# The input halves of the projections in one tile, two of eight pieces on the weights' place modulo 256 bytes

## The chip, the cores and the metric

The kernel runs on one core of a Trainium2 chip. The metric is the device time of one execution in microseconds; a measurement gives the median of several executions of the kernel before and of the kernel after on the same chip.

## The reference

Two transformer blocks are chained on a sequence of 256 tokens with 1024 features. The first has one layer: a mixer (gated delta rule and an S5 state-space model), cross-attention to a memory of 256 tokens, a SwiGLU feed-forward. The second has two layers: a self-attention (stick-breaking and MoBA heads in the first, forgetting attention in the second), a cross-attention to a second memory, a feed-forward with a short convolution. Cut to what the change touches:

```python
def memory_cross_attention(h, mem_h, w_q, w_kv, w_out):
    q = (h @ w_q).reshape(B, S, XA_HEADS, XA_HEAD_DIM)
    kv = (mem_h @ w_kv).reshape(B, M, 2, XA_HEADS, XA_HEAD_DIM)
    k, v = kv[:, :, 0], kv[:, :, 1]
    s = jnp.einsum('bshd,bmhd->bhsm', q, k).astype(jnp.float32) * (XA_HEAD_DIM ** -0.5)
    p = jax.nn.softmax(s, axis=-1).astype(h.dtype)
    o = jnp.einsum('bhsm,bmhd->bshd', p, v).reshape(B, S, XA_DIM)
    return o @ w_out

def conv_ffn(h, w_up, conv_w, conv_b, w_down):
    u = h @ w_up
    ...
    gate, val = c[..., :D_FF_2], c[..., D_FF_2:]
    return (jax.nn.silu(gate) * val) @ w_down
```

Everything is float32, and each block ends in a normalization.

## The kernel before

**Products in two halves.** A float32 product is made of three faster ones: each operand is split into a high half, rounded to the matmul's own float32 format (F32R), and a low half, the rest. `mm3` issues high by high, high by low, low by high into one accumulator. The normalized input of a layer is held by feature: eight pieces of 128 features by 256 tokens, in the tiles xh and xl (`new_x`, L466; `split_x` fills them piece by piece). Weights come from memory as 512 KB pieces (raw), ScalarE writes their high half (whi), VectorE their low half (wlo); `Weights.pump` keeps four such pairs ahead in the pool "weights", and from the second block on three more in "weights2" (L1685).

**Projections.** `proj_f` runs over the eight pieces k, with the weights as the operand held in TensorE and the pieces of xh and xl streamed: 24 matmuls of 128x256. `proj_t`, for the values, turns it round: the weights are streamed, the halves of x held.

```python
for k in range(KD):
    mm3(p, wh[:, k], wl[:, k], N.xh[:, k], N.xl[:, k], k == 0, k == KD - 1)
```

`out_mm` (L576) is the same product for output projections: oh and ol (an attention's result), ahl (a feed-forward's) or xh and xl (the mixer's, kept in x tiles) are streamed. A feed-forward part runs 22 times over gate (24 matmuls), up (24) and down (24). In the trace a row names the streamed operand first: mm<-xh,whi streams xh against whi.

**Places.** Within the 256-byte rows of a partition, xh, xl, the memory's halves (memh, meml, mem2h, mem2l), ahl, oh and ol start 128 bytes past a multiple of 256; each piece is 1024 bytes, so all pieces do. whi and wlo start 192 past it. So in projections and output products the streamed operand lies 64 bytes before the weights, modulo 256; in `proj_t` it is 64 behind. On the same place (distance 0) lie three kinds of products: the S5 gate (s5ghl at 192, against whi; 48 matmuls), the cross-attention's result (PT with xvh and xvl, all at 128; 48) and its scores (Q, K, lb and V, all at 128; 48). The tiles v1 (192 bytes in the pool main), "beside" and "beside2" set the starts of what follows them in their pools.

**Softmax.** `softmax` works on one head's scores in PSUM: VectorE takes the negative maximum (nm, L1536), in the memory attention also multiplied by the rows' scale (nm<-nm,rs), ScalarE the exponential with its sum (sm), VectorE the reciprocal (rc, L1546) and the scaling of P (L1548). `softmax_pair` does two heads at once. nm, sm and rc have three buffers each. `memory_attention` issues its steps in the order of a list, MEMORY: s0 to s3 are the heads' scores with their softmax, t the transposes, v the values' products, p the products with the values, w one piece of weights ahead. The order on each engine comes out of a list scheduler, under the limits that the buffers set.

Of the kernel before, what the change touches and what calls it, by code (L numbers as in the profile page):

```python
# [10 lines left out]
F32 = mybir.dt.float32  # L11
F32R = mybir.dt.float32r
# [7 lines left out]
S = 256  # L20
KD = D // 128
# [11 lines left out]

MEMORY = "s0 w1 s1 w1 s2 w1 s3 w1 v0 t0 w1 v1 t1 w1 p0 t2 w1 p1 x0 t3 w1 p2 p3 x1".split()

XK_AT = [("v", 1), ("z", 0), ("z", 1), ("z", 1)]
EPS = 1e-6
PI = math.pi
# [149 lines left out]
def behind(tc, later, earlier):  # L188

    tc.add_manual_dep(later, earlier.name, mybir.DependencyInfo(  # L190
        mybir.DependencyClass.NoSync, mybir.DependencyReason.DATA), reason="order")
# [38 lines left out]
def body(ctx, tc, I, out):  # L230
# [5 lines left out]
    const = ctx.enter_context(tc.tile_pool(name="const", bufs=1))  # L236
    wpool = ctx.enter_context(tc.tile_pool(name="weights", bufs=1))
    main = ctx.enter_context(tc.tile_pool(name="main", bufs=1))
    small = ctx.enter_context(tc.tile_pool(name="small", bufs=2))
    W = Weights(nc, wpool, 4, 4, lambda a, b: behind(tc, a, b))  # L240

    v1 = main.tile([128, 48], F32, name="v1")


    def cols(w, c0, c1):
        return w.rearrange("(k p) n -> p k n", p=128)[:, :, c0:c1]
# [6 lines left out]
    for nm in "ukqvz":  # L253
        for c in range(2):
            W.add((nm, c), cols(w_in, OFFS[nm] + 256 * c, OFFS[nm] + 256 * c + 256), split=nm not in "uk")
            for x, at in enumerate(XK_AT):
                if at == (nm, c):
# [58 lines left out]
    def mm():  # L316
        return bank("mm", banks["mm"])
# [8 lines left out]
    def halves(p):  # L326
        return p.rearrange("p (a s) -> p a s", a=2)
# [133 lines left out]
    N = State()  # L461
    N.pending = []
    N.by_feature = True
    N.last = None

    def new_x():  # L466
        N.xh = main.tile([128, KD, S], F32R, name="xh", tag="xh", bufs=1)
        N.xl = main.tile([128, KD, S], F32R, name="xl", tag="xl", bufs=1)

    def split_x(n, src, gcol):  # L470
        a = A.activation(N.xh[:, n], src[:, n], AF.Copy, scale=gcol)
# [114 lines left out]
    def residual(accs, gcol, fold=None, by_feature=True):  # L586


        h = hn = N.h
        N.by_feature = by_feature  # L590
        new_x()
        if fold is not None:
            gg = small.tile([128, KD], F32, name="gg", tag="gg", bufs=1)
# [104 lines left out]
    def layer_cols():  # L698
        for nm in ("mix", "xa", "mem", "ffn"):
            for l in range(2):  # L700
                COL[nm, l] = COL[nm + "2"][:, KD * l:KD * l + KD]

    N.h = hT = main.tile([128, KD, S], F32, name="h", tag="h", bufs=1)
    new_x()
    def transpose_in(dst, src, evac, bank):
        for kp in range(4):
# [39 lines left out]
    def tt(o, a, b, op):  # L746
        N.v = V.tensor_tensor(o, a, b, op=op).ins  # L747
# [558 lines left out]
    def fill(n=1):  # L1306
        for _ in range(n):
            if fills:
                fills.pop(0)()
# [77 lines left out]
    for n in range(4):  # L1387
        p = mm()
# [5 lines left out]
        if n == 1:  # L1394
            split_x32()
        W.pump(1)
    fin_v(lambda i, n: v1[:, 0:n] if i else const.tile([128, n], F32, name="v0"))
    layer_cols()
    mixed = []

    def mix():
        if not mixed:
            new_x()
            mixed.extend([N.xh, N.xl])
        return mixed
# [40 lines left out]
    def dn_step(i):  # L1446
        if dn.left and i >= dn.least:
            with lane("dn"):
                dn.least = next(dn_gen, None)
            if dn.least is None:  # L1450
                dn.left = False
# [17 lines left out]
    for i in range(18):  # L1469
# [7 lines left out]
        if i < 16:  # L1477
            nm, n = todo[i]
            p = mm()
# [9 lines left out]
        if i % 2:  # L1489
            fill(2 * XK_AT.count((nm, n // 2)) if i < 16 else 0)  # L1490
        dn_step(i)
# [13 lines left out]
    for c in (2, 3, 0):  # L1505
        for kk in range(2):
            k = 2 * c + kk
# [11 lines left out]


    pm = ctx.enter_context(tc.tile_pool(name="second", bufs=1))
    pm.tile([128, 32], F32, name="beside")
    kvT = pm.tile([128, 2, S], F32, name="kvT")
    kvv = pm.tile([128, 2, S], F32, name="kvv")

# [4 lines left out]
    def softmax(p, parts, rs=None):  # L1530

        P = pm.tile([128, 512], F32, name="P", tag="P", bufs=2)
        nm = small.tile([128, 2], F32, name="nm", tag="nm", bufs=3)
        sm = small.tile([128, 2], F32, name="sm", tag="sm", bufs=3)
        if parts[0].stop - parts[0].start == parts[1].stop - parts[1].start:
            V.tensor_reduce(nm, halves(p), axis=AX.X, op=OP.max, negate=True)  # L1536
        else:
            for t, q in enumerate(parts):
                V.tensor_reduce(nm[:, t:t + 1], p[:, q], axis=AX.X, op=OP.max, negate=True)
        if rs is not None:  # L1540
            tt(nm, nm, rs, OP.mult)
        for t, q in enumerate(parts):
            A.activation(P[:, q], p[:, q], AF.Exp, bias=nm[:, t:t + 1], accum_out=sm[:, t:t + 1],
                         scale=1.0 if rs is None else rs[:, t:t + 1])
        rc = small.tile([128, 2], F32, name="rc", tag="rc", bufs=3)
        V.reciprocal(rc, sm)  # L1546
        for t, q in enumerate(parts):
            TS(P[:, q], P[:, q], rc[:, t:t + 1], None, op0=OP.mult)  # L1548
        return P

    def softmax_pair(p):

        P = pm.tile([128, 2, 384], F32, name="P", tag="P", bufs=2)
        nm = small.tile([128, 2, 2], F32, name="nm4", tag="nm4", bufs=3)
        sm = small.tile([128, 2, 2], F32, name="sm4", tag="sm4", bufs=3)
        for t in range(2):
            V.tensor_reduce(nm[:, t], p[t], axis=AX.X, op=OP.max, negate=True)
        for t, q in enumerate(CAUSAL):
            for i in range(2):
                A.activation(P[:, i, q], p[t][:, i], AF.Exp, bias=nm[:, t, i:i + 1], accum_out=sm[:, t, i:i + 1])  # L1560
        rc = small.tile([128, 2, 2], F32, name="rc4", tag="rc4", bufs=3)
        V.reciprocal(rc, sm)
        for t, q in enumerate(CAUSAL):
            for i in range(2):
                TS(P[:, i, q], P[:, i, q], rc[:, t, i:i + 1], None, op0=OP.mult)
        return P
# [81 lines left out]
    def x_scores(i):  # L1648
        p = full_scores([(qs[i][a][:, c], ks[i][b][c]) for c in range(2) for a, b in ((0, 0), (0, 1), (1, 0))])
        if i == 0:  # L1650
            flush()
            w_["rs"] = row_scale(1.0 / 16)
        Ps[i] = softmax(p, FULL, w_["rs"])
# [29 lines left out]
    residual(accs, COL["ffn"])  # L1683
    px_cm.__exit__(None, None, None)
    W.more = (ctx.enter_context(tc.tile_pool(name="weights2", bufs=1)), 3)  # L1685
    W.more[0].tile([128, 16], F32, name="beside2")
    padded = ctx.enter_context(tc.tile_pool(name="padded", bufs=1))
    W.nextra = 2
    W.extra = lambda: main.tile([128, 2048], F32, name="raw4", tag="m8", bufs=3)
# [192 lines left out]
    class Group:  # L1882


        def __init__(self, l, g, kind):
            self.l, self.g, self.kind = l, g, kind
            self.w = {}
            self.bank = acc if g < 3 else mm
# [130 lines left out]
    def memory_attention(l, gcol):  # L2019
# [17 lines left out]
        def score(h):  # L2037
            c, r = head(h)
            w["P", h] = softmax(full_scores([(w["q"][r, c], kvT[r, c])], acc), FULL, rs)
# [110 lines left out]
    v = small.tile([128, 2], F32, name="var", tag="var", bufs=2)  # L2150
    TS(v, ps[:, 0:2], 1.0 / D, EPS, op0=OP.mult, op1=OP.add)
    r = rsqrt_small(v, 2, A)
    for t in range(2):
        o = main.tile([128, D], F32, name="ofin", tag="m8", bufs=3)
# [31 lines left out]
```

## Time and profile before

| | |
|---|---|
| three executions | 1195.25, 1197.91, 1200.18 us (median 1197.91) |
| the profiled execution | 1196.38 us |
| its span, first to last instruction | 1194.6 us |
| TensorE (PE) busy | 97% of the span |
| VectorE, ScalarE, GpSimd busy | 75%, 56%, 6% |
| share of the chain that ended last on PE | 83% |

Matmuls are pipelined: a row's 0.28 us is the stay of one matmul in the engine, and the next one starts about 0.11 us after it. What a matmul costs in a stretch is therefore the distance of starts. The column PEclk is the clock that TensorE was granted, as a share of 2.4 GHz.

### The profile page before, as it was taken

To read this page: it belongs to the slowest core of one execution; us is meant where nothing else is said; L and a number is where in the kernel's file an instruction comes from. 1 tells how busy PE (TensorE), PEld (TensorE's weight loads), DVE (VectorE), ACT (ScalarE), POOL (GpSimd) and SP (SyncE) were. 2 spreads that over 40 slices of the span, in tenths; PEclk is the share of its full clock that TensorE was granted. 3 is DMA by queue.
4 is the path that set the end of the run, shared out by engine and by line. 5 is a ranking of instruction groups with operands and counts; after the bars stand their busy time and mean duration, and the time that the engine had idled before them with its cause. 6 is when DMAs were issued, how large, how long until landed. Compare 5 with 4: busy or idle time off the path is not lost.

```text
span 1194.6 us, 24101 instructions
## 1 busy us (share of the span) xinstructions
PE 1156.8 (97%) x9720; PEld 1102.7 (92%) x9720; DVE 891.8 (75%) x1682; ACT 667.1 (56%) x1155; POOL 77.1 (6%) x175
## 2 busy tenths in 40 slices
PE   8999998999999999999998999999999999999998
PEld 6798888999999999988797999999988888999998
DVE  8899747866875565877876899877765686978775
ACT  6553345655644444756665665655454666655653
POOL 1425300100000000200000000000100000000000
PEclk9999899999999999999999999999999999999998
DMA  8733352746665665653353576665543464666530
GB/s 207 198 83 109 98 159 63 220 150 188 194 198 169 195 198 163 185 169 118 105 168 113 162 208 194 195 212 158 145 140 116 143 172 137 179 190 195 176 90 36
DMA packets 262017, 188.01 MB, mean 157 GB/s; under 512 B 20143, under 2 KB 246852, under 8 KB 261906
## 3 DMA queue, kind: packets, MB, share of 16 engines
q1 hardware_dynamic: 258034, 185.23, 52.9%
q8 instruction: 76, 1.25, 0.4%
q10 hardware_dynamic: 3568, 0.86, 0.3%
q0 software_dynamic: 304, 0.39, 0.3%
q14 instruction: 35, 0.29, 0.1%
HBM read 183.70 MB, written 2.75 MB: 156 GB/s over the span
## 4 chain that ended last, share of the span: by engine, by line
PE 83%; DVE 7%; DMA 4%; ACT 2%; issue 1%; POOL 1%; SPq 0%; ACTq 0%; DVEq 0%; POOLq 0%
PE mm L536 16%; PE mm L537 16%; PE mm L538 16%; PE acc L582 7%; PE acc L584 7%; PE acc L583 7%; DVE wlo L157 1%; PE acc L1995 1%; DMA raw<-in_w_in_dram 1%; DVE s5a L747 1%; DVE ca L1110 1%; PE acc L1866 1%; DMA s5u<-uT 1%; DMA raws<-in_w_out_dram 1%; ACT whi L137 1%
## 5 line engine op out<-in xcount | busy, mean ns | idle before, releaser
L157 DVE TENSOR_TENSOR wlo<-raw,whi 128x1024 fp32r<-128x1024 f32 x322 | 392.0, 1226 | 149.6 <-ACT whi L137 147.3
L137 ACT ACTIVATE whi<-raw 128x1024 fp32r<-128x1024 f32 x322 | 337.0, 1057 | 285.6 <-PE mm L537 106.2
L536 PE MATMUL mm<-xh,whi 128*128 128x256 f32 x1504 | 421.3, 281 | 2.3 <-ACT V L218 1.4
L537 PE MATMUL mm<-xl,whi 128*128 128x256 f32 x1504 | 420.1, 280 | 0.0
L538 PE MATMUL mm<-xh,wlo 128*128 128x256 f32 x1504 | 419.7, 279 | 0.0
L536 PEld LDWEIGHTS mm<-xh,whi 128*128 128x128 f32 x1504 | 283.4, 189 | 4.3 <-ACT V L218 1.5
L537 PEld LDWEIGHTS mm<-xl,whi 128*128 128x128 f32 x1504 | 282.8, 188 | 1.5 <-issue 1.0
L538 PEld LDWEIGHTS mm<-xh,wlo 128*128 128x128 f32 x1504 | 283.6, 189 | 0.3
L584 PE MATMUL acc<-ahl,wlo 128*128 128x256 f32 x528 | 144.8, 279 | 0.4 <-DVE wlo L157 0.4
L583 PE MATMUL acc<-ahl,whi 128*128 128x256 f32 x528 | 144.9, 279 | 0.0
L582 PE MATMUL acc<-ahl,whi 128*128 128x256 f32 x528 | 141.7, 279 | 0.2 <-ACT ahl L218 0.2
L584 PEld LDWEIGHTS acc<-ahl,wlo 128*128 128x128 f32 x528 | 99.2, 189 | 0.8 <-DVE wlo L157 0.8
L583 PEld LDWEIGHTS acc<-ahl,whi 128*128 128x128 f32 x528 | 98.9, 188 | 0.0
L582 PEld LDWEIGHTS acc<-ahl,whi 128*128 128x128 f32 x528 | 97.2, 189 | 0.5 <-ACT ahl L218 0.5
L1740 DVE SCALAR_TENSOR_TENSOR gu<-pad,cwc,gu 128x256 f32<-128x256 f32 x176 | 75.1, 478 | 3.4 <-ACT gu L218 3.4
L582 PE MATMUL acc<-oh,whi 128*128 128x256 f32 x224 | 61.8, 284 | 0.9 <-ACT oh L218 0.9
L584 PE MATMUL acc<-oh,wlo 128*128 128x256 f32 x224 | 61.9, 279 | 0.0
L583 PE MATMUL acc<-ol,whi 128*128 128x256 f32 x224 | 61.7, 278 | 0.0
L218 ACT ACTIVATE gu<-pad,cwc 128x256 f32<-128x256 f32 x88 | 47.5, 590 | 14.7 <-DVE pad L747 14.6
L582 PEld LDWEIGHTS acc<-oh,whi 128*128 128x128 f32 x224 | 41.3, 188 | 2.5 <-ACT oh L218 1.9
L584 PEld LDWEIGHTS acc<-oh,wlo 128*128 128x128 f32 x224 | 42.1, 188 | 1.1 <-issue 1.1
L583 PEld LDWEIGHTS acc<-ol,whi 128*128 128x128 f32 x224 | 42.2, 188 | 0.4 <-issue 0.4
(537 smaller groups left out, 1951.7 us busy)
## 6 DMA issues: line engine op xcount, KB each, us to landing
raw<-in_ffn_w_up_dram SPq DMA_DIRECT2D x88, 512.0 KB
raw<-in_ffn_w_down_dram SPq DMA_DIRECT2D x44, 512.0 KB
raw<-in_ab_w_in_dram SPq DMA_DIRECT2D x24, 512.0 KB
raw<-in_fox_w_in_dram SPq DMA_DIRECT2D x24, 512.0 KB
raw<-in_w_gate_dram SPq DMA_DIRECT2D x22, 512.0 KB
raw<-in_w_up_dram SPq DMA_DIRECT2D x22, 512.0 KB
raw<-in_w_down_dram SPq DMA_DIRECT2D x22, 512.0 KB
raw<-in_w_in_dram SPq DMA_DIRECT2D x20, 512.0 KB
```

Of the source, the lines that this page charges most:

```text
L137: i_ = self.nc.scalar.activation(hi, src, AF.Copy)
L157: i_ = self.nc.vector.tensor_tensor(lo, src, hi.bitcast(F32), op=OP.subtract)
L218: i = self.nc.scalar.activation(out, in_, func, **kw)
L536: T.matmul(p, lhsT=wh, rhs=xh, start=start, stop=False, **kw)
L537: T.matmul(p, lhsT=wh, rhs=xl, start=False, stop=False, **kw)
L538: T.matmul(p, lhsT=wl, rhs=xh, start=False, stop=stop, **kw)
L582: T.matmul(p, lhsT=wh[:, kk, c], rhs=xh, start=first and n % 2 == 0, stop=False, skip_group_check=True)
L583: T.matmul(p, lhsT=wh[:, kk, c], rhs=xl, start=False, stop=False, skip_group_check=True)
L584: T.matmul(p, lhsT=wl[:, kk, c], rhs=xh, start=False, stop=last, skip_group_check=True)
L747: N.v = V.tensor_tensor(o, a, b, op=op).ins
L1110: STT(a, c[:, i:i + S], w(i), a, op0=OP.mult, op1=OP.add)
L1740: STT(t[:, i], u[:, i, d:d + S], cw(d, j + NH * i), t[:, i], op0=OP.mult, op1=OP.add)
```

## The change

Both halves of a layer's input go into one tile x. Pieces 0 and 1 of both halves stand first, then 64 bytes are left out, then pieces 2 to 7. The class Part maps a piece to its place. The tile v1 is dropped (its contents go into a tile of the pool const), and the pads "beside" and "beside2" become "gap" and "gap2" with other sizes. By these, in the kernel after, whi and wlo of both pools start 128 past a multiple of 256, pieces 0 and 1 of x 128 as well, and pieces 2 to 7, the memory's halves, ahl, oh, ol and s5ghl 192. So the streamed operand is 64 behind the weights, and in pieces 0 and 1 of x on the same place; the S5 gate's products are no longer on the same place, the cross-attention's scores and result still are. nm, sm and rc (and the four-column ones of `softmax_pair`) have two buffers in place of three.

```diff
+XK = 2
...
-    v1 = main.tile([128, 48], F32, name="v1")
...
+    class Part:
+        def __init__(self, t, i):
+            self.t, self.i = t, i
+
+        def __getitem__(self, key):
+            k, n = key[1], 1
+            if isinstance(k, slice):
+                k, n = k.start, k.stop - k.start
+                assert k >= XK or k + n <= XK
+            o = (self.i * XK + k) * S if k < XK else (2 * XK + self.i * (KD - XK) + k - XK) * S + 16
+            v = self.t[key[0], o:o + n * S]
+            if isinstance(key[1], slice):
+                return v.rearrange("p (k s) -> p k s", k=n)
+            return v[:, key[2]] if len(key) > 2 else v
+
     def new_x():
-        N.xh = main.tile([128, KD, S], F32R, name="xh", tag="xh", bufs=1)
-        N.xl = main.tile([128, KD, S], F32R, name="xl", tag="xl", bufs=1)
+        t = main.tile([128, 2 * KD * S + 16], F32R, name="x", tag="x", bufs=1)
+        N.xh, N.xl = Part(t, 0), Part(t, 1)
...
-    fin_v(lambda i, n: v1[:, 0:n] if i else const.tile([128, n], F32, name="v0"))
+    fin_v()
...
-    pm.tile([128, 32], F32, name="beside")
+    pm.tile([128, 16], F32, name="gap")
...
-        nm = small.tile([128, 2], F32, name="nm", tag="nm", bufs=3)
-        sm = small.tile([128, 2], F32, name="sm", tag="sm", bufs=3)
+        nm = small.tile([128, 2], F32, name="nm", tag="nm", bufs=2)
+        sm = small.tile([128, 2], F32, name="sm", tag="sm", bufs=2)
...
-        rc = small.tile([128, 2], F32, name="rc", tag="rc", bufs=3)
+        rc = small.tile([128, 2], F32, name="rc", tag="rc", bufs=2)
...
-    W.more[0].tile([128, 16], F32, name="beside2")
+    W.more[0].tile([128, 48], F32, name="gap2")
```

The instructions on TensorE, ScalarE, GpSimd and SyncE and their order are the same before and after. On VectorE the order differs in the two memory attentions alone. In the first one, before, VectorE's rows from head 1's maximum to head 1's scaling are these (nm the maxima, rc the reciprocals, P the exponentials):

```order
L1536 TENSOR_REDUCE nm<-acc 128x2
L747 TENSOR_TENSOR nm<-nm,rs 128x2
L1536 TENSOR_REDUCE nm<-acc 128x2
L1546 RECIPROCAL rc<-sm 128x2
L747 TENSOR_TENSOR nm<-nm,rs 128x2
L1548 TENSOR_SCALAR P<-P,rc 128x256 x2
L1536 TENSOR_REDUCE nm<-acc 128x2
L1546 RECIPROCAL rc<-sm 128x2
L747 TENSOR_TENSOR nm<-nm,rs 128x2
L1548 TENSOR_SCALAR P<-P,rc 128x256 x2
```

The second maximum, head 2's, stands ahead of head 0's reciprocal, and its product with the scale ahead of head 0's scaling. The same place of VectorE after:

```order
L1552 TENSOR_REDUCE nm<-acc 128x2
L763 TENSOR_TENSOR nm<-nm,rs 128x2
L1562 RECIPROCAL rc<-sm 128x2
L1552 TENSOR_REDUCE nm<-acc 128x2
L1564 TENSOR_SCALAR P<-P,rc 128x256 x2
L763 TENSOR_TENSOR nm<-nm,rs 128x2
L1562 RECIPROCAL rc<-sm 128x2
L1552 TENSOR_REDUCE nm<-acc 128x2
L1564 TENSOR_SCALAR P<-P,rc 128x256 x2
L763 TENSOR_TENSOR nm<-nm,rs 128x2
```

Head 0's reciprocal moved ahead of head 2's maximum, which now stands between it and head 0's scaling; head 1's and head 3's likewise. The second memory attention has the same.

## Rows read from the trace of the kernel before

**Rows 1.** The page's engines (busy us, share, instructions), and the list of cores.

```profile
PE 1156.8 (97%) x9720; PEld 1102.7 (92%) x9720; DVE 891.8 (75%) x1682; ACT 667.1 (56%) x1155; POOL 77.1 (6%) x175
...
core 0: 1194.6 us, clock 0.987
```

**Rows 2.** Windows, PE, in three feed-forward parts: us, busy (matmuls), PEclk, DMA share, GB/s.

```profile
340.00:470.00 130.00, 130.00 (x1106) 1.00 0.64 189
680.00:810.00 130.00, 130.00 (x1149) 1.00 0.67 196
1040.00:1170.00 130.00, 130.00 (x1106) 1.00 0.51 155
```

**Rows 3.** Timeline of PE, cross-attention's output: start us, us, engine, line, operation, out<-in, shapes.

```profile
283.83 0.28 PE L582 MATMUL acc<-oh,whi 128*128 128x256 f32 x1
...
286.89 0.28 PE L536 MATMUL mm<-PT,xvh 128*128 128x256 f32 x1
287.01 0.28 PE L582 MATMUL acc<-oh,whi 128*128 128x256 f32 x1
...
288.42 0.28 PE L537 MATMUL mm<-PTl,xvh 128*128 128x256 f32 x1
...
289.62 0.28 PE L538 MATMUL mm<-PT,xvl 128*128 128x256 f32 x1
289.74 0.28 PE L582 MATMUL acc<-oh,whi 128*128 128x256 f32 x1
...
290.33 0.28 PE L584 MATMUL acc<-oh,wlo 128*128 128x256 f32 x1
```

**Rows 4.** Timeline of PE, cross-attention: memory projections, scores, projections of x, of memory.

```profile
223.37 0.39 PE L536 MATMUL mm<-whi,memh 128*128 128x256 f32 x2
...
228.81 0.28 PE L1581 MATMUL mm<-V,Q 128*128 128x256 f32 x1
...
230.69 0.28 PE L536 MATMUL mm<-xh,whi 128*128 128x256 f32 x1
...
236.22 0.28 PE L538 MATMUL mm<-xh,wlo 128*128 128x256 f32 x1
...
236.46 0.28 PE L537 MATMUL mm<-wlo,memh 128*128 128x256 f32 x1
...
241.88 0.28 PE L538 MATMUL mm<-whi,meml 128*128 128x256 f32 x1
```

**Rows 5.** Timeline of PE, from the S5 gate into the mixer's output.

```profile
187.55 0.28 PE L536 MATMUL mm<-s5ghl,whi 128*128 128x256 f32 x1
...
187.91 0.29 PE L582 MATMUL s<-xh,whi 128*128 128x256 f32 x1
...
188.27 0.28 PE L582 MATMUL s<-xh,whi 128*128 128x256 f32 x1
...
189.40 0.28 PE L583 MATMUL s<-xl,whi 128*128 128x256 f32 x1
```

**Rows 6.** Windows, PE, over thirteen stretches: the longest, and the sum of all.

```profile
670.50:825.50 155.00, 155.00 (x1370) 1.00 0.66 194
...
sum 313.80, PE 313.80; mean PE 24.14
```

**Rows 7.** Groups by line and shape, PE: count, busy us, mean ns, idle before.

```profile
L536 PE MATMUL mm<-xh,whi 128*128 128x256 f32 x1504 | 421.3, 281 | 2.3 <-ACT V L218 1.4 <-ACT xh L218 0.9
...
L536 PE MATMUL mm<-whi,xh 128*128 128x256 f32 x128 | 36.6, 286 | 0.2 <-DVE pd L1924 0.2
```

**Rows 8.** Timeline of all engines in the first memory attention; brackets: idle before, releaser.

```profile
631.75 0.68 DVE L1536 TENSOR_REDUCE nm<-acc 128x2 f32<-128x512 f32 x1
...
632.37 0.17 DVE L1546 RECIPROCAL rc<-sm 128x2 f32<-128x2 f32 x1
...
632.57 0.61 DVE L1548 TENSOR_SCALAR P<-P,rc 128x256 f32<-128x256 f32 x2
...
632.98 0.33 PE L1588 MATMUL mm<-ident,P 128*128 128x128 f32 x1 [1.96 <-DVE P L1548]
```

More of the change, by code (lines that the diff above doesn't have):

```diff
@@ L1553, in softmax_pair @@
         P = pm.tile([128, 2, 384], F32, name="P", tag="P", bufs=2)
-        nm = small.tile([128, 2, 2], F32, name="nm4", tag="nm4", bufs=3)
-        sm = small.tile([128, 2, 2], F32, name="sm4", tag="sm4", bufs=3)
+        nm = small.tile([128, 2, 2], F32, name="nm4", tag="nm4", bufs=2)
+        sm = small.tile([128, 2, 2], F32, name="sm4", tag="sm4", bufs=2)
         for t in range(2):
@@ L1560, in softmax_pair @@
                 A.activation(P[:, i, q], p[t][:, i], AF.Exp, bias=nm[:, t, i:i + 1], accum_out=sm[:, t, i:i + 1])
-        rc = small.tile([128, 2, 2], F32, name="rc4", tag="rc4", bufs=3)
+        rc = small.tile([128, 2, 2], F32, name="rc4", tag="rc4", bufs=2)
         V.reciprocal(rc, sm)
```

## The prediction

> **What bounds the kernel now.** I read the page's table of engines and the list of cores first. TensorE is busy 1156.8 of 1194.6 us, at a mean granted clock of 0.987 [rows 1]. So there are only some 38 us in which it does nothing, and a change that leaves its instructions alone can move the time in two ways: by those gaps, or by the pace at which the same matmuls follow each other. The second is the larger. I therefore cut a long stretch out of each of the three feed-forward parts, where TensorE never idles [rows 2]. All three have the same shapes, the same 130.00 us of busy time and a granted clock of 1.00 (the upper of the two levels, 2.4 GHz), but 1106, 1149 and 1106 matmuls. Adding the 0.28 us by which the last one overhangs, a matmul starts every 130.28/1106 = 117.8 ns in the first and third, every 130.28/1149 = 113.4 ns in the second. Same clock, same code, 4.4 ns apart: there are two paces, and TensorE keeps one for whole stages.
>
> The timeline shows a third one and what goes with it [rows 3]. From 283.83 to 286.89 us lie 27 starts, 113.3 ns each: the fast pace. At 286.89 one matmul of PT with xvh stands between the others. Both its streamed operand and the weights loaded under it lie 128 bytes past a multiple of 256; I call such a matmul coincident. After it, 287.01 to 288.42 has 12 starts of 117.5 ns: the slow pace. From 288.42 to 289.62 there are only coincident ones, 10 starts of 120 ns. From 289.74 on it is 118 ns again. So a coincident matmul takes 120 ns at a distance of 0, and the reader should see that what counts more is the pace that is left behind.
>
> **The change part by part.**
>
> *Which matmuls become coincident.* Pieces 0 and 1 of xh and xl now share their place modulo 256 with the weights; each piece takes three matmuls. The page counts 1504 matmuls of the first product with xh streamed and 128 with xh as the weights' side [rows 7], at 8 to a projection 188 + 16 = 204 projections, so 204 x 6 = 1224 coincident matmuls, six in a row at the head of each. With w_out's first 512 rows, whose pieces 0 and 1 enter output products (2 x 8 x 3 = 48), that makes 1272. The 48 products of s5ghl, now coincident, stop being so.
>
> *Their own price.* Against the slow pace each costs 120 - 117.8 = 2.2 ns, 1272 x 2.2 = **+2.8 us**. The bounds: 0, if the conflict hides under another limit, and 1272 x (120 - 113.3) = 8.5 against the fast pace. I take the lower reference, since I expect the slow pace around them (next step). s5ghl gives back 48 x 2.2 = 0.1 us.
>
> *The pace behind them.* This is the main term. In the trace are eight runs of three and more coincident matmuls, the first at 180 us and the last in [rows 3]. Seven are followed by the slow pace, one by the fast one [rows 5]: 187.55 to 187.91 at 120 ns, then 188.27 to 189.40 with 10 starts of 113. Five of the seven were slow before the run as well, so they show only that a run doesn't lift the slow pace. The others start fast: from 223.37 to 228.81 there are 48 starts of 113.3 ns, then the scores with their coincident products, and from 230.69 to 236.22 there are 47 of 117.7 [rows 4]; and the loss at 286.89 [rows 3]. The kernel after leaves each run by a step of the streamed operand from 128 to 192. The nearest to that is 236.34 in [rows 4], where projections of xh (128) are followed by those of the memory (192): slow before, and slow after, 46 starts from 236.46 to 241.88 in 5.42 us, 117.8 ns. I take it that a run of six leaves the slow pace behind, at each of the 204 projections.
>
> What this costs is what now goes fast behind a projection's first pieces. Thirteen longer fast stretches hold 313.80 us and, by the counts of their rows, 2802 starts; the longest is the second feed-forward part with 1370 [rows 6]. All but some 420 of these (output products ahead of the first projection after an interruption, and the last window) lie behind a coincident run after the change: 2350 x 4.4 = 10.4 us. Shorter fast pieces, which I counted only roughly in the timeline, are a third as many again (some 900), half of them behind a run: 500 x 4.4 = 2.2. Together **+12.6 us**, between 0 (a run leaves the pace as it found it) and 16.5 (every fast start of both counts flips). The feed-forward parts that are slow stay so.
>
> *VectorE in the memory attention.* With two buffers in place of three for the softmax columns, the reciprocal of head 0 stands ahead of the maximum of head 2, and so the maximum stands between it and the scaling of P. In the trace the maximum takes 0.68 us, ran at 631.75 while VectorE waited for the sum, the reciprocal came at 632.37, the scaling at 632.57, and TensorE, which had waited 1.96 us for this P, went on at 632.98 [rows 8]. Now the maximum begins behind the reciprocal and the scaling about 0.6 us later. Head 2's own score waits for nothing earlier. Queued behind it are head 1's reciprocal and scaling and head 2's exponentials on ScalarE; they slip by the same 0.6. TensorE has nothing else queued ahead of these transposes, so the 0.6 is on the path, in each of two layers: **+1.2 us**, from 0 (the values' matmuls between the heads take it up) to 2.5 (each pair of heads loses it again). A gain is excluded, since the scaling can't precede the reciprocal.
>
> *At nothing:* the tile v1 (its columns go into another tile of the same size by the same transfers), the pads, and the single tile for both halves of x. All rows on the other engines keep their order; were the single tile to make a reader of xl wait for a writer of xh, the xl split follows its xh split within a microsecond anyway.
>
> *Sum:* 2.8 - 0.1 + 12.6 + 1.2 = 16.5 us. The profiled execution took 1196.38 us, 1.8 above its span and 1.5 under the median of 1197.91; 1196.4 + 16.5 = **1213 us**. Its own range: 0.5 to 8.5 for the coincident ones' price, 10 to 14 for the pace (the rough count), 0 to 2.5 for VectorE, which don't all meet at one end: 1208 to 1219.
>
> **The rivals.** *The run of six lifts TensorE onto the fast pace.* For it: [rows 5], where it does, and the single crossing at 223.25, just ahead of [rows 4], behind which the fast pace held. Then the head of every projection resets the pace, and feed-forward parts one and three, now slow, gain. About 480 us of the span go at the slow pace, 260 of them in [rows 2]; 480 x (1 - 113.3/117.8) = -18.3; the coincident ones then cost 1272 x 6.7 = +8.5 against the fast pace; VectorE +1.2: -8.6, so 1188 us, with 1184 to 1194 around it. It decides itself at the step from piece 1 to piece 2: it needs that step to come out fast in more than about half of the projections. Against it: seven of eight runs, and 236.34 in the direction that matters.
>
> *The pace isn't touched.* What switches it may be only interruptions, since most changes of pace in the trace stand at an idle time or another shape. Then only the coincident ones cost, 1272 x (120 - 115.7, the middle of the paces) = +5.5, with VectorE 1203 us.
>
> *The place costs nothing.* [Rows 3] show 10 coincident starts at 120 ns, but at most 2.2 ns off the slow pace, which could be the shape's own. Then only VectorE's 1.2 remains: 1197.6 us. The Trainium skill speaks for this one: SBUF — State Buffer, "Who interferes with whom", gives TensorE two independent read ports, one for the moving operand and one for the weights, and by "The single rule" names only the pair shared by VectorE and GpSimd as contended; by that the place of two TensorE operands can't matter, and the sum would be the VectorE term alone. The three paces at one clock in [rows 2, 3] speak against it, since nothing else in these stretches differs.
>
> **How the numbers follow.** A measurement of this kernel tells about 0.5% (6 us) from no change. The forecast 0.58; the lift onto the fast pace 0.25; the untouched pace 0.09 (half of it over the 6 us); no cost of places 0.08. Faster 0.25, same 0.12, slower 0.63. The forecast and the two milder cases leave out 0.25 and the forecast's tails, so the range must reach into the lift: 1187 to 1219; the likeliest case alone is 1208 to 1219.
>
> **What would show it.** The window 680 to 810 (shifted by what comes ahead of it) should hold some 1103 matmuls in place of 1149: 130.28/118.2, one matmul in six being coincident; the other two windows about 1102. By the lift all three would hold about 1137 (130.28/114.6); by the untouched pace 1149 would fall to 1138 and 1106 to 1102. In the timeline the six first matmuls of a projection should start 120 ns apart and those behind at 117 to 118. TensorE's wait for P in the memory attention should grow from 1.96 to about 2.6 us. The forecast is wrong if starts of 113 ns follow the sixth matmul of most projections.

## The result and the profile after

| | before | after |
|---|---|---|
| executions | 6, 1190.10 to 1201.26 us | 6, 1211.06 to 1218.83 us |
| median | 1197.93 us | 1212.99 us |
| ratio to before | | 1.0141, 95% interval 1.0102 to 1.0179 |
| the profiled execution, its span | 1196.38, 1194.6 us | 1218.83, 1217.0 us |

The change costs 15 us, 1.4%. The profiled execution of the kernel after is the slowest of its six, 5.8 us above their median; where that lies, the stages show. They are cut at the first column sum (acc<-ones,sums) in each feed-forward part, read in the timeline; the third column is the kernel of experiment e1_none, below.

| stage, us | before | after | e1_none |
|---|---|---|---|
| to the sum in the first feed-forward part | 312.9 | 319.3 | 315.1 |
| to that of the second | 350.2 | 355.2 | 352.6 |
| to that of the third | 345.3 | 355.4 | 354.0 |
| to the end | 186.2 | 187.1 | 186.6 |

Ten of the 22.4 us between the two spans lie in the third row, which holds the second feed-forward part almost whole. The 6.5 us of the first row are partly that execution's own: its longest wait for the first memory, 4.9 us, was 1.4 before, and the clock granted in its first 200 us was 0.93 against 0.96. The page and the cores of the kernel after:

```profile
PE 1176.4 (97%) x9720; PEld 1122.2 (92%) x9720; DVE 892.6 (73%) x1682; ACT 667.3 (55%) x1155; POOL 78.7 (6%) x175
...
core 0: 1217.0 us, clock 0.983
```

TensorE's busy time grows by 1176.4 - 1156.8 = 19.6 us with the same 9720 instructions; no other engine's grows by over 1.6 us [rows 1]. Part of the 19.6 can be that execution's lower clock: 0.983 over the span, where before had 0.987. The same windows as in [rows 2], after (us, busy, matmuls, granted clock, DMA share, GB/s):

```profile
340.00:470.00 130.00, 130.00 (x1098) 1.00 0.63 184
680.00:810.00 130.00, 130.00 (x1100) 1.00 0.65 190
1040.00:1170.00 130.00, 130.00 (x1102) 1.00 0.60 178
```

All three feed-forward parts now go at about one matmul in 118.2 to 118.7 ns (130.28 divided by the count), where the second one had 113.4. One projection's head in that part, in the timeline of TensorE (start us, us, engine, line, operation, out<-in):

```profile
720.64 0.28 PE L598 MATMUL acc<-ahl,whi 128*128 128x256 f32 x1
...
723.35 0.28 PE L600 MATMUL acc<-ahl,wlo 128*128 128x256 f32 x1
723.46 0.29 PE L552 MATMUL mm<-x,whi 128*128 128x256 f32 x1
...
724.19 0.28 PE L552 MATMUL mm<-x,whi 128*128 128x256 f32 x1
724.31 0.28 PE L553 MATMUL mm<-x,whi 128*128 128x256 f32 x1
...
726.31 0.29 PE L552 MATMUL mm<-x,whi 128*128 128x256 f32 x1
```

From 720.64 to 723.35 there are 23 starts of 118 ns, from 723.46 to 724.19 the six coincident ones, 122 ns each with the steps into and out of them, from 724.31 to 726.31 again 17 of 118. It is slow ahead of the head and slow behind it.

### The profile page after: what moved, and what is told of

Its sections match the earlier page's. It is cut to its first block, busy times and chain, and to the rows that moved or that the text cites. A ratio compares the mean times of both kernels' runs of the same rounds, so it can differ in the third digit from the quotient of the medians.

```text
span 1217.0 us, 24102 instructions
## 1 busy us (share of the span) xinstructions
PE 1176.4 (97%) x9720; PEld 1122.2 (92%) x9720; DVE 892.6 (73%) x1682; ACT 667.3 (55%) x1155; POOL 78.7 (6%) x175
## 4 chain that ended last, share of the span: by engine, by line
PE 86%; DVE 7%; ACT 2%; DMA 2%; POOL 1%; issue 1%; DVEq 0%; ACTq 0%; POOLq 0%
PE mm L552 16%; PE mm L553 16%; PE mm L554 16%; PE acc L598 7%; PE acc L600 7%; PE acc L599 7%; PE mm L1395 1%; DVE wlo L158 1%; DMA raw<-in_w_in_dram 1%; PE acc L2011 1%; DVE s5a L763 1%; PE acc L1882 1%; DVE ca L1126 1%; ACT whi L138 1%; PE spare L552 1%
## 5 line engine op out<-in xcount | busy, mean ns | idle before, releaser
L552 PE MATMUL mm<-x,whi 128*128 128x256 f32 x1504 | 424.5, 283 | 2.2 <-ACT V L219 1.2
L554 PE MATMUL mm<-x,wlo 128*128 128x256 f32 x1504 | 421.9, 281 | 0.0
L553 PE MATMUL mm<-x,whi 128*128 128x256 f32 x1504 | 421.8, 281 | 0.0
L552 PEld LDWEIGHTS mm<-x,whi 128*128 128x128 f32 x1504 | 283.2, 189 | 4.2 <-ACT V L219 1.4
L553 PEld LDWEIGHTS mm<-x,whi 128*128 128x128 f32 x1504 | 282.7, 188 | 1.4 <-issue 1.0
L554 PEld LDWEIGHTS mm<-x,wlo 128*128 128x128 f32 x1504 | 282.6, 188 | 0.3
L763 DVE TENSOR_TENSOR pad<-mm,rb 128x512 f32<-128x512 f32 x44 | 30.1, 689 | 18.8 <-PE mm L554 18.8
```

Source lines behind the costliest of these rows:

```text
L552: T.matmul(p, lhsT=wh, rhs=xh, start=start, stop=False, **kw)
L553: T.matmul(p, lhsT=wh, rhs=xl, start=False, stop=False, **kw)
L554: T.matmul(p, lhsT=wl, rhs=xh, start=False, stop=stop, **kw)
```

## The experiments

All are compared with runs of the kernel before on the same chip. A place is an address modulo 256 bytes, "behind" and "before" are distances of the streamed operand from the weights' place. The windows and timelines are of one execution of each kernel, the times and ratios of all.

### No coincident piece: e1_none

```diff
-XK = 2
+XK = 0
```

> The kernel after with XK = 0: no piece of x on the weights' place, all streamed tiles 64 bytes behind the weights, softmax columns double as in the kernel after. Theory (the six coincident matmuls at a projection's head leave TensorE at the slow pace): nothing resets the pace, so it is mixed as in the kernel before, about 1197.9 + 1.2 = 1199 us (1193 to 1204), and whole feed-forward parts go at one pace, 113.3 or 117.8 ns. Rival (the distance of +64 bytes is slow by itself, the coincident pieces only add their own price): about 1211 us, and all three feed-forward parts at 117.8 ns.

Measured: 1210.6 us, ratio 1.0128 (1.0098 to 1.0159). Windows in the three parts (as all windows from here on, 130 us in the first part and 110 in the others; 936 in 110.00 us is 117.8 ns a matmul, 973 is 113.3, 964 is 114.4, 932 is 118.3):

```profile
340.00:470.00 130.00, 130.00 (x1106) 1.00 0.64 189
700.00:810.00 110.00, 110.00 (x936) 1.00 0.63 190
1060.00:1170.00 110.00, 110.00 (x936) 1.00 0.58 173
```

The rival's figure, to a microsecond. With nothing coincident in the projections the loss is nearly all there, and all three parts are slow. So the theory that the coincident run is what takes the pace down falls as an explanation of the loss: 64 bytes behind is enough (in what way, e7_seed_behind tells). What the pieces add is the difference of the two ratios, 0.13%, or 1.6 us (2.4 between the medians); the intervals of the two ratios overlap, so by the times it is not told from nothing. The windows show it: 936 matmuls here, 933 and 932 in the same windows of the kernel after.

### The same pieces, left by a step down: e2_below

```diff
-            o = (self.i * XK + k) * S if k < XK else (2 * XK + self.i * (KD - XK) + k - XK) * S + 16
+            o = (self.i * XK + k) * S if k < XK else (2 * XK + self.i * (KD - XK) + k - XK) * S + 48
...
-        t = main.tile([128, 2 * KD * S + 16], F32R, name="x", tag="x", bufs=1)
+        t = main.tile([128, 2 * KD * S + 48], F32R, name="x", tag="x", bufs=1)
...
-    W.more[0].tile([128, 48], F32, name="gap2")
+    W.more[0].tile([128, 16], F32, name="gap2")
```

> The kernel after with the same two coincident pieces, but all other streamed tiles 64 bytes before the weights instead of 64 behind (pad in x 48 floats, gap2 16). A run is then left by a step of the streamed operand of 64 bytes down, as from the S5 gate into the mixer's output in the trace of before, where the fast pace followed. Theory, with the pace set by the direction of that step: fast behind each projection's head, about 1188 us (1184 to 1194), 113.3 ns in all three feed-forward parts outside the first six matmuls. Rival (any coincident run leaves the slow pace): 1213 us as the kernel after. Rival (only the price of the coincident matmuls counts): about 1204 us.

Measured: 1193.15 us, ratio 0.9973 (0.9951 to 0.9995).

```profile
340.00:470.00 130.00, 130.00 (x1138) 1.00 0.65 195
700.00:810.00 110.00, 110.00 (x964) 1.00 0.65 193
1060.00:1170.00 110.00, 110.00 (x964) 1.00 0.50 149
```

The same 1272 coincident matmuls, and all three parts are fast. The two parts that were slow before gain, the second one pays for its coincident matmuls (964 instead of 973). Counted over the timeline, of 142 coincident runs with a clear pace ahead and behind, 134 are followed by the fast pace, some 10 of them out of the slow one; in the kernel after it is 3 of 144. A run does set the pace, and which one depends on the places. The eight others here are five of the six heads of the values' projections (`proj_t`, where the weights are streamed), a run of the cross-attention, which lies on 64 here, and two runs of four, of heads that other work splits in four and two. The three of the kernel after are a run of the cross-attention, on 192 there, and again two runs of four. The time lies 5 us above what the theory gave. To the sum in the first feed-forward part the profiled execution took 314.8 us, 1.9 more than before; where the rest lies is not shown.

### The softmax columns alone: e3_columns

```diff
+    small.tile([128, 48], F32, name="gap", bufs=1)
...
-        nm = small.tile([128, 2], F32, name="nm", tag="nm", bufs=3)
+        nm = small.tile([128, 2], F32, name="nm", tag="nm", bufs=2)
...
```

The same goes for sm, rc and the four-column ones.

> The kernel before with only the softmax columns double (a tile of 48 floats keeps every place as it was). Theory: the maximum of the next head stands ahead of the scaling in the two memory attentions, +1.2 us (0 to 2.5): 1199.1 us; TensorE's wait for the first P there grows from 1.96 to about 2.6 us. Rival (hidden): no change.

Measured: 1198.14 us, ratio 1.0018 (0.9994 to 1.0041): between no change and the 1.2 us this doesn't decide. The wait does; TensorE's waits on VectorE for P, in both memory attentions (us in total, times, longest), before and here:

```profile
PE mm L1588 <- DVE P L1548: 3.9, 2, 2.0
PE mm L1589 <- DVE P L1549: 4.8, 2, 2.4
```

and in the kernel after, with VectorE's rows at the place of [rows 8]:

```profile
PE mm L1604 <- DVE P L1564: 4.9, 2, 2.4
```

```profile
642.67 0.17 DVE L1562 RECIPROCAL rc<-sm 128x2 f32<-128x2 f32 x1 [0.53 <-ACT P L219]
642.75 0.67 DVE L1552 TENSOR_REDUCE nm<-acc 128x2 f32<-128x512 f32 x1
643.34 0.61 DVE L1564 TENSOR_SCALAR P<-P,rc 128x256 f32<-128x256 f32 x2
643.74 0.33 PE L1604 MATMUL mm<-ident,P 128*128 128x128 f32 x1 [2.43 <-DVE P L1564]
```

The maximum now lies between the reciprocal and the scaling: 0.67 us from one to the other where it was 0.20, and the first wait is 2.43 instead of 1.96.

### All eight pieces coincident: e4_all

```diff
-XK = 2
+XK = 8
```

> The kernel after with XK = 8: all eight pieces of x on the weights' place, 204 x 24 = 4896 coincident matmuls instead of 1272; the feed-forward's down products still 64 behind. Theory (2.2 ns each against the slow pace, and the slow pace behind them): 1213 + 3672 x 2.2 = 1221 us. Rival (the whole 15 us of the change is the price of 1272 coincident matmuls, 11.8 ns each): about 1256 us.

Measured: 1224.66 us, ratio 1.0238 (1.0207 to 1.0269); 925 matmuls in the second window, 119.2 ns each. 3672 more coincident matmuls cost 1224.66 - 1212.99 = 11.7 us, 3.2 ns each: somewhat above the 2.2 of the prediction, and far from 11.8. By the window it is 2.1: 119.2 against the 117.8 ns of e1_none, with two in three of the part's matmuls coincident.

### Six extra matmuls on the higher place, on the lower place: e5_seed_high, e6_seed_low

Both are the kernel before, 64 before the weights, with this ahead of the seventh gate projection of each part; e6_seed_low has `lhsT=N.xh[:, 0, 0:128], rhs=N.xh[:, 1]` in the matmul.

```diff
             p = mm()
+            if j == 6:
+                wh, wl = W.get((tag, "g", j // 2), j % 2)
+                for i in range(6):
+                    T.matmul(p[:, :S], lhsT=wh[:, 0], rhs=wh[:, 2:4], start=True, stop=True)
             proj_f(p[:, :S], (tag, "g", j // 2), j % 2)
```

> The kernel before with six extra matmuls of whi against whi (both on 192, the higher of the two places of a projection; their result is overwritten) ahead of the seventh gate projection of each feed-forward part. New theory: TensorE keeps whichever pace it has until a coincident run or an interruption; a run on the higher of the two places leaves the fast pace, one on the lower the slow pace. Then feed-forward parts one and three go fast behind the extra matmuls: 140 and 126 us at 113.3 instead of 117.8 ns, -5.3 - 4.8, the extra ones +18 x 0.12 = 2.2: 1196.4 - 7.9 = 1188.5 us. Rival (a short run sets nothing, in e2_below the repetition or the neighbours did it): 1198.6 us.

> As e5_seed_high, but the six extra matmuls stream xh against xh (both on 128, the lower of the two places). New theory: the slow pace behind them, so feed-forward part two, fast in the kernel before, loses 126 us x 4.4/113.3 = +4.9, and the extra ones +2.2: 1203.5 us; parts one and three stay slow. Rival (any coincident run leaves the fast pace where the streamed operands stand 64 before the weights): 1188.5 us.

Measured: 1188.08 us, ratio 0.9945 (0.9923 to 0.9967), and 1207.65 us, ratio 1.0121 (1.0076 to 1.0165). Windows of the first, then of the second:

```profile
340.00:470.00 130.00, 130.00 (x1147) 1.00 0.66 195
700.00:810.00 110.00, 110.00 (x973) 1.00 0.65 193
1060.00:1170.00 110.00, 109.88 (x970) 1.00 0.49 144
```

```profile
340.00:470.00 130.00, 130.00 (x1105) 1.00 0.63 188
700.00:810.00 110.00, 110.00 (x937) 1.00 0.64 190
1060.00:1170.00 110.00, 110.00 (x936) 1.00 0.56 170
```

Six matmuls, 0.7 us, decide over the 130 us that follow in the first part of e5_seed_high. Its second and third part were at 113 ns ahead of them already, and in the second other work splits them after the fourth: 118 ns behind four, 113 behind the last two. That first part in the timeline:

```profile
346.56 0.28 PE L584 MATMUL acc<-ahl,wlo 128*128 128x256 f32 x1
...
348.68 0.28 PE L584 MATMUL acc<-ahl,wlo 128*128 128x256 f32 x1
348.80 0.88 PE L1762 MATMUL mm<-whi 128*128 128x256 f32 x6
349.51 0.28 PE L536 MATMUL mm<-xh,whi 128*128 128x256 f32 x1
...
349.87 0.28 PE L536 MATMUL mm<-xh,whi 128*128 128x256 f32 x1
...
351.91 0.28 PE L536 MATMUL mm<-xh,whi 128*128 128x256 f32 x1
```

Ahead of them 18 starts of 118 ns, behind them, after three starts of 120 that settle it, 18 of 113.3 (349.87 to 351.91). In e6_seed_low the second part was at 113 ns up to its extra matmuls and at 118 from them on. So a run doesn't lead to one pace always; it matters on which of the two places it lies. In the third part, which the profiled execution of e6_seed_low entered fast, they had the same effect; the first was slow ahead of them. Its time is 4 us above the figure forecast. To the sum in the first part, ahead of every extra matmul, the profiled execution took 316.9 us where before took 312.9, so the excess need not lie with them.

### The same, 64 behind: e7_seed_behind

The kernel of e1_none with e5's edit and `lhsT=N.xh[:, 0, 0:128], rhs=N.xh[:, 1]`.

> e1_none (all streamed tiles 64 behind the weights, nothing coincident) with six extra matmuls of x against x (both on 192, here the higher place). New theory: the fast pace behind them in all three feed-forward parts, -15 + 2.2: 1210.6 - 12.8 = 1198 us, so 64 behind isn't slow by itself, only entered slow. Rival (64 behind holds the slow pace): 1212.8 us, all three parts at 117.8 ns.

Measured: 1198.27 us, ratio 1.0033 (1.0003 to 1.0063).

```profile
340.00:470.00 130.00, 130.00 (x1146) 1.00 0.66 195
700.00:810.00 110.00, 110.00 (x973) 1.00 0.65 194
1060.00:1170.00 110.00, 110.00 (x973) 1.00 0.52 154
```

As expected: 64 behind holds the fast pace as well as 64 before does, and here the six turned all three parts from 118 to 113 ns. What e1_none lost in these parts, it lost by entering them slow. The time comes back to that of before because the first and the third part, slow there, are fast here; other stretches stay slow.

Runs that belong to the kernels tell the same. The cross-attention's coincident runs lie on 128 in the kernel before, the lower of its two places, and on 192 in e1_none, the higher. Before, all seven of ten and more with a pace behind them are followed by the slow one; in e1_none all seven by the fast one, such as this, which came out of the slow one (20 starts of 118 ns ahead, 18 of 113 behind):

```profile
269.91 0.28 PE L552 MATMUL mm<-whi,memh 128*128 128x256 f32 x1
...
272.27 0.28 PE L554 MATMUL mm<-whi,meml 128*128 128x256 f32 x1
...
274.16 0.28 PE L598 MATMUL acc<-oh,whi 128*128 128x256 f32 x1
...
276.20 0.28 PE L598 MATMUL acc<-oh,whi 128*128 128x256 f32 x1
```

### 128 bytes apart: e8_far

```diff
-            o = (self.i * XK + k) * S if k < XK else (2 * XK + self.i * (KD - XK) + k - XK) * S + 16
+            o = (self.i * XK + k) * S if k < XK else (2 * XK + self.i * (KD - XK) + k - XK) * S + 32
...
-    W.more[0].tile([128, 48], F32, name="gap2")
+    W.more[0].tile([128, 32], F32, name="gap2")
```

On e1_none (the tile x grows by 16 columns too).

> e1_none with all streamed tiles 128 from the weights (pad in x 32 floats, gap2 32; the S5 gate's products coincident again, as in the kernel before). It tells how the distance bears on the pace that is entered after interruptions. If 64 behind is the odd one: mixed, 1196 to 1202 us. If every other distance than 64 before is slow: 1210 us. If it is always fast: 1181 us.

Measured: 1219.22 us, ratio 1.0209 (1.0171 to 1.0247), slower than any of the three cases.

```profile
340.00:470.00 130.00, 130.00 (x1098) 1.00 0.61 189
700.00:810.00 110.00, 110.00 (x929) 1.00 0.62 189
1060.00:1170.00 110.00, 110.00 (x919) 1.00 0.57 175
```

At 128 apart the matmuls go at 118.7 ns and, in the third part, at 120.0, the price of coincident ones.

### The extra matmuls in the kernel after: e9_after_seed

The kernel after with e7's edit, but pieces 2 and 3 of x in the extra matmuls (on 192).

> The kernel after (two coincident pieces, on 128, the lower place) with the six extra matmuls of e7_seed_behind (x against x, both on 192, the higher place) ahead of the seventh gate projection of each feed-forward part. Prediction's step (a projection's six coincident matmuls leave the slow pace, also where it was fast): fast only from the extra matmuls to the head of the next projection, slow from there on: 1213 + 2.2 = 1215 us, and the three parts at one matmul every 118.1 ns. Rival (the distance of 64 behind decides alone what is entered, the coincident pieces only cost their 2.2 ns; once fast it stays fast as in e7_seed_behind): 1198.3 + 2.4 = 1201 us.

Measured: 1218.02 us, ratio 1.0149 (1.0121 to 1.0178).

```profile
340.00:470.00 130.00, 130.00 (x1099) 1.00 0.62 184
700.00:810.00 110.00, 110.00 (x932) 1.00 0.65 185
1060.00:1170.00 110.00, 110.00 (x932) 1.00 0.59 174
```

The figure of the prediction's step, 3 us over, and far from the rival's. But in all three parts the extra matmuls met coincident ones of x at once, so the run says little of them. A fast stretch came in the third part alone, behind the last four of a split head (1048.70 to 1050.40 us, 15 starts of 113.3 ns), and the kernel after has such stretches without extra matmuls. The step itself is seen there, ahead of the first sum:

```profile
313.49 0.28 PE L552 MATMUL mm<-x,whi 128*128 128x256 f32 x1
...
315.42 0.28 PE L554 MATMUL mm<-x,wlo 128*128 128x256 f32 x1
315.53 0.28 PE L552 MATMUL mm<-x,whi 128*128 128x256 f32 x1
...
316.25 0.28 PE L552 MATMUL mm<-x,whi 128*128 128x256 f32 x1
...
317.78 0.28 PE L553 MATMUL mm<-x,whi 128*128 128x256 f32 x1
```

17 starts of 113.5 ns, then the six coincident matmuls of the next head, and from 316.25 on 13 of 118. So in the kernel after a projection's head takes the fast pace away, as predicted; it finds it in few places only, since TensorE is slow ahead of nearly all heads.

### Two and one extra matmul: e10_seed2, e11_seed1

```diff
-                for i in range(6):
+                for i in range(2):
```

This is against e5_seed_high; e11_seed1 has `range(1)`.

> e5_seed_high with two extra matmuls in place of six at each of the three places. If two are enough to leave the fast pace: 12 x 0.12 = 1.4 us less than there, 1186.6 us. If it takes more: parts one and three stay slow, 1196.4 + 0.7 = 1197 us.

> e5_seed_high with one extra matmul in place of six. In the trace of before a single coincident matmul was followed by either pace. If one is enough: 1188.1 - 15 x 0.12 = 1186.3 us; if what comes ahead decides: parts one and three, slow before it, stay slow, 1196.4 + 0.4 = 1196.8 us.

Measured: 1195.86 us, ratio 0.9990 (0.9969 to 1.0011), and 1196.51 us, ratio 0.9983 (0.9954 to 1.0013): neither differs from before. Windows of e10_seed2 and then of e11_seed1:

```profile
340.00:470.00 130.00, 130.00 (x1147) 1.00 0.66 195
700.00:810.00 110.00, 110.00 (x936) 1.00 0.66 190
1060.00:1170.00 110.00, 110.00 (x973) 1.00 0.49 144
```

```profile
340.00:470.00 130.00, 130.00 (x1106) 1.00 0.64 189
700.00:810.00 110.00, 110.00 (x973) 1.00 0.66 194
1060.00:1170.00 110.00, 110.00 (x973) 1.00 0.49 144
```

Two made the first and the third part, slow up to them, fast, and the second, fast up to them (113 ns), slow: each time the other pace. One left all three as it found them, slow, fast and fast. Both profiled executions, 1189.66 and 1189.65 us, are the fastest of ten, so their windows don't stand for the medians. What so short a run leaves depends on the pace ahead of it. Runs of two and of four elsewhere, parts of split heads in the kernel after, e2_below and e9_after_seed, do the same: with a clear pace ahead and behind, all 12, these three included, turned it.

## Why the prediction was right, and where it wasn't

*What bounds the kernel.* Right: between the two profiled executions the gaps moved by a few microseconds, TensorE's busy time by nearly 20, part of it perhaps by the clock [rows 1, 2].

*The coincident ones' price.* 2.2 ns each and 2.8 us; measured 1.6 to 2.4 us for 1272 (kernel after against e1_none, within the noise), and 3.2 ns each for the 3672 more of e4_all by the times, 2.1 by its window. The right term; the bound against the fast pace (8.5 us) was rightly not taken. The earlier text puts s5ghl on 192 in the kernel after; it lies on 64. Either way it is off the weights' place.

*The pace behind them.* The size was right, the cause only half. Forecast were 1103 matmuls in the second part's window and 1102 in the others; there are 1100, and 1098 and 1102. The 12.6 us agree with e1_none's 1.28% (15 us) less the columns' 1 to 2. But e1_none has no run at the projections' heads and loses about the same. The step that failed is the one that laid the loss to the run of six ("I take it that a run of six leaves the slow pace behind"): the run does that (141 of 144 in the kernel after, at 315.53 out of the fast pace), but the kernel with its tiles 64 behind enters its parts slow without it. I had left out that the distance itself was changed for every matmul, and treated 64 before and 64 behind alike because both paces occur at either. The comparison that would have told them apart was not in the trace of before: there no long stretch of projections runs at 64 behind. The change at 236.34 that stood for it has no coincident run and moves both operands' places. And the one run in eight that was followed by the fast pace, the S5 gate's, was the only one on the higher place (192); the other seven lie on 128. So the exception was half of the rule.

*VectorE.* 0.6 us a layer and 1.2 in all were forecast; the wait for P went from 3.9 to 4.9 us in all, so 1.0. That the whole time moves by it is not shown (e3_columns, 0.9994 to 1.0041).

*The sum* of 1213 us is met by the median of 1212.99, which is partly luck: the kernel before scatters by some 10 us between executions, and the term of 12.6 us was laid to the run, while the distance alone gives a loss of that size. What coincident heads would cost in a kernel that enters its parts fast, no run shows.

*The rivals.* The lift onto the fast pace did not happen, and e2_below shows what it needs: the same pieces, but the rest of x before the weights' place. There the 1193 us lie at the end of the rival's 1184 to 1194. The price of 1203 us for an untouched pace fell with the windows. That places cost nothing fell with e1_none and e8_far: the Trainium skill's table of ports (SBUF — State Buffer, "Who interferes with whom") has TensorE's two operands on independent ports, and by it none of these kernels would differ beyond VectorE's microsecond and the extra matmuls' two. The measurement decides: 1.28% for e1_none and 2.09% for e8_far against before.

*What stays open:* why, at 64 behind, TensorE enters every part slow after an interruption, while at 64 before it enters some fast and some slow (the third part slow in the kernel before, fast in e11_seed1 ahead of its extra matmul). The runs show that it does, at three parts in e1_none and in e7_seed_behind ahead of the extra matmuls, not by what.

## What to carry to other kernels

Read the distance of starts, not the busy share: an engine at 97% busy and at full clock can still run 4% below its pace, and a stretch of one shape tells it by its count of matmuls alone. Before a loss is laid to the new pieces of a layout, run the layout without them; here one number settled it. Where two paces exist and the engine keeps the one it has, a handful of matmuls that set it is cheap: e5_seed_high spends 2.2 us and is 0.55% faster than the kernel before.

## What was not expected of the hardware

- With the same shape, clock and code a 128x256 matmul starts every 113.3 or 117.8 ns where its two operands lie 64 bytes apart modulo 256, every 118.7 or 120.0 at 128 apart (e8_far), and about 120 on the same place; it keeps the pace over more than a thousand matmuls.
- A run of six on one place sets the pace of what follows at 64 apart: on the higher of the two places fast (all three runs of e7_seed_behind, two of e5_seed_high; 134 of 142 runs in e2_below), on the lower slow (e6_seed_low, 3 of 3; 141 of 144 in the kernel after). "Higher" is not the whole rule: in e2_below five of six heads of the values' projections lie on the higher place and leave the slow pace. Beyond the places tried (64, 128 and 192) nothing is shown.
- Runs of two and four such matmuls leave the pace that they did not find (12 of 12). One left the pace as it was in e11_seed1 (3 of 3); the single one of [rows 3] is followed by the slow pace, out of the fast one.
